# Stationary blocks made contiguous, value products by pairs of heads, and later statistics in a four-block transformer kernel

## The chip, the cores and the metric

The kernel runs on 1 core of a Trainium2 chip. The metric is the device time of one execution in microseconds (us). The kernel before was timed three times: 1725.38, 1725.91 and 1728.11 us, median 1725.91 us.

## The reference, cut to what matters

A sequence of 256 tokens of width 1024, batch 1, in float32, goes through four blocks: a forgetting attention block ("fox"), a block with three sparse attention branches ("nsa"), a block with stick-breaking and dilated attention and a gated feed-forward part ("mixer2", "ffn2"), and a block with pooling, attention and a product-key expert layer ("mixer3", "peer"). Heads have 64 columns; fox and mixer2 have 16 heads. What the change touches:

```python
# fox: every head; c is the running sum of log_sigmoid(f + b_f)
logits = q @ k.T * scale + c[:, None] - c[None, :]        # causal
o = softmax(logits) @ v;   y = (o * silu(z)) @ w_out

# nsa: compress 32 tokens (stride 16) to one key and one value per group
blk = x[16 * i : 16 * i + 32] + pe                        # 32 x 64, flattened to 2048
kc = silu(blk @ w1) @ w2                                  # w1: 2048 x 256

# mixer2, heads 0..7 stick-breaking, 8..15 softmax with a distance bias
log_stay = where(key < query, log_sigmoid(-z), 0)
w = exp(log_sigmoid(z) + sum of log_stay over later keys);  o = w @ v
o = rms_norm_of_each_head(o) * gain
```

All of it starts with a root-mean-square norm of x (in fox: `h = x * rsqrt(mean(x*x)) * g`).

## The kernel before, in words

**Products.** Activations lie transposed in SBUF: 128 rows of a 128-column chunk by 256 tokens (`S`). A float32 product of full accuracy is three float32r products: each operand is split into a high part (rounded to float32r) and a low part (what is left), and hi*hi, hi*lo and lo*hi are summed in PSUM (`mm3`, L448 to L452). Where an operand is handed to TensorE as plain float32, as in `attn_av` (L593 to L596) and in transposes, TensorE makes two passes of it, which are two records in the trace.

**Weights.** `Weights` streams 504 chunks of 128 x 1024 float32 (512 KB): the SP queue loads them into four buffers (`wraw`), ACT makes `whi` (L241), DVE makes `wlo` (L242). There are three pairs of `whi`/`wlo`, and a fourth from another pool for every fourth chunk. `next()` asks for the split of two chunks beyond the one used. In nsa the transfers of `rope` (L632, L633) go through the same SP queue. During mixer2 the queue also brings 48 chunks of `ada`, which DVE reduces (L291), 16 of them among the 16 chunks of the query and key projection.

**Order of the work.** Each stage is a Python generator; `weave` steps the projections ("main") and, at a rate, the attention ("side"), so that TensorE has matmuls of the next weights while a head goes through its softmax. The list so made is then ordered on every engine by the framework's planner, which takes the ready instruction of the earliest place, by its own cost estimates; on the chip each engine runs its list in order. PSUM has four names of two banks each: "pj", "s", "t", "o".

**fox** (0 to 170 us). The projection of the 16 gate columns (`proj(1)`, bank "pj") is evicted by `f_evac` (L666), which first calls `stats()` (L648): ACT squares eight tiles, POOL adds them up (L655), TensorE sums over partitions with a matrix of ones (L657), ACT takes the root, `cols` turns it into a column by two transposes (L444). Then come a few small operations on 16 partitions and, in `c3`, the decay as three bf16 parts. The values follow (`proj_nat(2)`, 8 chunks, banks "s" and then "pj", matmuls of 512 columns, L496 to L498), evicted by ACT (`v_evac`, L696) into `vN` in float32. Then queries and keys are projected in 8 steps of two chunks (`qk_evac`, L701, into one tile for all heads; `stack`, L522, builds float32r operands). For each head `attn_scores` (L548) makes four float32r matmuls and two bf16 ones of 128 and 256 columns that add the decay (L556; the stationary operand is one column of `sel`, repeated 128 times), softmax and norm run on DVE and ACT, three transposes go to PSUM (L584 to L586), DVE copies them out (`ptw`, L588), `attn_av` multiplies by 64 columns of `vN`, and after each odd head `gated` (L605) multiplies by the gate and splits.

**nsa** (170 to 368 us). `blocks()` (L809) adds the position table to `Z`, in which the 8 places of a block lie next to each other, and splits the sum into `zh` and `zl`. `compress` (L824) takes, for each of 16 places j, every eighth column from j on as stationary operand (L830) and multiplies it with 256 columns of `w1` in three products (L832 to L834): 2 x 16 x 3 = 96 matmuls over 8 weight chunks.

**mixer2** (368 to 486 us). Values as in fox (L1070), then the 8 steps of queries and keys woven with 16 heads. A stick-breaking head has two bf16 matmuls of 128 columns for the mask (L1119), a chain of ACT and DVE operations, two float32 matmuls with a triangle (L1136, L1137) and an exponential straight to `ptw` (L1139) without transposes; a dilated head goes as in fox, with its norm on POOL. `finish` (L1083) copies the pair out of PSUM, squares, sums by head on TensorE, and splits. mixer3 has attention too, with `attn_av` as it is.

Of the kernel before, what the change touches and what calls it, by code (L numbers as in the profile page):

```python
# [270 lines left out]
def program(tc, A, out, upto=99):  # L271
    nc = tc.nc
    ctx = ExitStack()
    with ctx:
# [322 lines left out]

        def resid(nxt):
# [42 lines left out]
        def fox(st1):  # L641
            sel = ph.tile([P, NH], BF, name="sel")
# [20 lines left out]
            c3 = ph.tile([P, S], BF, name="c3")  # L663
            nc.vector.memset(c3, 0.0)

            def f_evac(c0, p, m):  # L666
# [16 lines left out]
                for i in range(3):  # L683
                    sl = c3[32 * i:32 * i + NH, :]
                    nc.vector.tensor_copy(sl, r)
                    if i < 2:
                        b = ph.tile([NH, S], F32, name="f6", bufs=2)
                        nc.vector.tensor_copy(b, sl)
# [4 lines left out]
            vN = ph.tile([P, 2, D], F32, name="vN")  # L693
# [4 lines left out]
            qk = ph.tile([P, 8, 2, S], F32, name="qk")  # L698

            def qk_evac(c0, p, m):  # L700
                nc.vector.tensor_tensor(qk[:, c0 // 2], p, rqk, op=OP.mult)  # L701
                stacks[c0 // 2] = stack(qk[:, c0 // 2, 0, :], qk[:, c0 // 2, 1, :])
                cnt["qk"] = c0 // 2 + 1
# [5 lines left out]
            def fox_attn():  # L709
                st = {}  # L710
                po = {}
                for i in range(NH + 3):
# [10 lines left out]
                    if 2 <= i <= NH + 1:  # L723
                        h = i - 2
                        if h % 2 == 0:
                            po[h // 2] = ps.tile([P, S], F32, name="o")
                        attn_av(po[h // 2][(h % 2) * 64:(h % 2) * 64 + 64, :], st[h],
                                lambda kb: vN[:, kb, h * 64:h * 64 + 64])
                        if h % 2 == 1:
                            while cnt["z"] <= h // 2:  # L730
                                yield
                            gated(og, h // 2, po[h // 2], sz)
                        yield

            drain(proj(1, hx, f_evac))
# [14 lines left out]
        def nsa(st1):  # L750
# [58 lines left out]
            def blocks():  # L809
                his = ph.tile([P, 2, 1040], F32R, name="zh", tag="bufA")  # L810
                los = ph.tile([P, 2, 1040], F32R, name="zl", tag="bufB")
                for ab in range(2):
                    t = ph.tile([P, 1040], F32, name="zt", bufs=2)
                    for n, w in ((0, 512), (1, 528)):
                        nc.vector.tensor_tensor(
                            t[:, 512 * n:512 * n + w].rearrange("p (c j) -> p c j", j=8),
                            Z[:, 512 * n:512 * n + w].rearrange("p (c j) -> p c j", j=8),
                            pek[:, n, ab * 8:ab * 8 + 8][:, None, :].to_broadcast([P, w // 8, 8]), op=OP.add)
# [228 lines left out]
        def mixer2(st1):  # L1047
# [19 lines left out]
            vN = ph.tile([P, 2, D], F32, name="vN")  # L1067

            def v_evac(c, tb, p):
                nc.scalar.mul(vN[:, tb, c * 512:c * 512 + 512], p, rc[:, tb:tb + 1])  # L1070

            qk = ph.tile([P, 8, 2, S], F32, name="qk")

            def qk_evac(c0, p, m):
                c = c0 // 2
                nc.vector.tensor_tensor(qk[:, c], p, rqk[:, c // 4], op=OP.mult)
                q, k = qk[:, c, 0, :], qk[:, c, 1, :]
# [5 lines left out]
            def finish(c, po):  # L1083
                o = ph.tile([P, S], F32, name="fo", bufs=2)
                nc.scalar.copy(o, po)
                sq = wk.tile([P, S], F32, name="sq")
                nc.scalar.activation(sq, po, AF.Square)
# [9 lines left out]
            def attn():  # L1097
                st, po = {}, {}

                def av(h):  # L1100
                    if h % 2 == 0:
                        po[h // 2] = ps.tile([P, S], F32, name="o")
                    attn_av(po[h // 2][(h % 2) * 64:(h % 2) * 64 + 64, :], st[h],
                            lambda kb: vN[:, kb, h * 64:h * 64 + 64])
                    if h % 2 == 1:
                        finish(h // 2, po[h // 2])

                for i in range(19):
                    if i < 16:
# [22 lines left out]
                    if 1 <= i <= 16:  # L1132
                        h = i - 1
                        if h < 8:
# [9 lines left out]
                    if 2 <= i <= 17:  # L1144
                        av(i - 2)
# [569 lines left out]
```

## Time and profile before

| | |
|---|---|
| median of 3 runs (lowest, highest) | 1725.91 us (1725.38, 1728.11) |
| the profiled execution's own time | 1728.64 us |
| its span, first to last instruction | 1726.9 us |
| mean granted TensorE clock | 0.993 |
| PE busy | 1680.3 us, 97% |
| weight loads (PEld) busy | 1545.8 us, 90% |
| DVE busy | 1294.4 us, 75% |
| ACT busy | 959.2 us, 56% |
| POOL busy | 185.7 us, 11% |
| read from HBM | 296 MB, 172 GB/s over the span |

Busy time is the time in which an engine had at least one instruction under way. TensorE pipelines matmuls, so the record of one matmul (0.28 us for 256 columns) is longer than the distance to the next; how fast it goes is read from the distance between starts. A bracket behind a row of the timeline tells how long the engine was idle before it and what ended the idle time.

### The profile page before, as it was taken

What the parts mean: (1) busy time and instruction counts of PE and PEld (TensorE: products, weight loads), DVE (VectorE), ACT (ScalarE), POOL (GpSimd) and SP (SyncE); (2) the same over time, 40 slices, a digit from 0 to 9 for tenths busy, and PEclk for the clock granted to TensorE, in tenths of its full rate; (3) what the DMA queues carried; (4) which work ended last, traced back from release to release, by engine and by line L of the source; (5) the groups of instructions that cost most, each with busy time, mean ns of one, the idle gap of its engine ahead of it and who ended that gap; (6) DMA issues with size and microseconds to landing.
All of it is one profiled execution on the core that took longest, in us unless ns stands there. A gap on an engine that the chain in (4) does not pass through costs nothing.

```text
span 1726.9 us, 31770 instructions
## 1 busy us (share of the span) xinstructions
PE 1680.3 (97%) x12108; PEld 1545.8 (90%) x12108; DVE 1294.4 (75%) x2691; ACT 959.2 (56%) x1813; POOL 185.7 (11%) x198
## 2 busy tenths in 40 slices
PE   8999999999999999999999999999999999999997
PEld 6999897788879999889989999999999988888886
DVE  5787767788867766777667987888999666666665
ACT  5666555656855545566644555554444555555554
POOL 2000133531130000111037000000000000000000
PEclk9999999999999999999999999999999999999999
DMA  6434542177527777434544454444444555555553
GB/s 229 144 125 150 170 144 93 63 251 267 190 99 242 258 260 244 138 128 169 186 157 163 163 163 163 158 157 156 161 160 154 173 193 195 195 194 191 193 192 120
DMA packets 84089, 300.08 MB, mean 174 GB/s; under 512 B 10144, under 2 KB 11040, under 8 KB 83680
## 3 DMA queue, kind: packets, MB, share of 16 engines
q1 hardware_dynamic: 83360, 296.39, 51.4%
q8 instruction: 95, 1.56, 0.4%
q10 hardware_dynamic: 576, 1.66, 0.3%
q14 instruction: 58, 0.48, 0.1%
HBM read 296.04 MB, written 1.05 MB: 172 GB/s over the span
## 4 chain that ended last, share of the span: by engine, by line
PE 52%; DVE 3%; ACT 1%; issue 0%; POOLq 0%; POOL 0%; DVEq 0%; ACTq 0%
PE s L1592 10%; PE t L1592 10%; PE pj L450 5%; PE pj L451 5%; PE pj L452 5%; PE o L1552 3%; PE s L450 2%; PE t L450 2%; PE s L452 2%; PE s L451 2%; PE t L451 2%; PE t L452 2%; DVE wlo L242 1%; PE s L1401 0%; PE o L595 0%
## 5 line engine op out<-in xcount | busy, mean ns | idle before, releaser
L242 DVE TENSOR_TENSOR wlo<-wraw,whi 128x1024 fp32r<-128x1024 f32 x486 | 601.9, 1241 | 194.1 <-ACT whi L241 192.3
L241 ACT CAST whi<-wraw 128x1024 fp32r<-128x1024 f32 x504 | 528.6, 1051 | 385.6 <-PE pj L451 124.4
L450 PE MATMUL pj<-hxh,whi 128*128 128x256 f32 x1456 | 422.8, 291 | 5.7 <-ACT vN L1070 1.9
L452 PE MATMUL pj<-hxh,wlo 128*128 128x256 f32 x1456 | 412.3, 284 | 1.9 <-DVE wlo L242 1.4
L451 PE MATMUL pj<-hxl,whi 128*128 128x256 f32 x1456 | 413.1, 284 | 0.6 <-DVE hxl L1161 0.4
L450 PEld LDWEIGHTS pj<-hxh,whi 128*128 128x128 f32 x1456 | 278.2, 191 | 14.0 <-issue 4.8
L452 PEld LDWEIGHTS pj<-hxh,wlo 128*128 128x128 f32 x1456 | 277.5, 191 | 3.8 <-DVE wlo L242 2.2
L451 PEld LDWEIGHTS pj<-hxl,whi 128*128 128x128 f32 x1456 | 277.8, 191 | 2.3 <-DVE hxl L1161 1.1
L1592 PE MATMUL s<-whi,hxl 128*128 128x512 f32 x512 | 157.8, 389 | 0.0
L1592 PE MATMUL t<-whi,hxl 128*128 128x512 f32 x512 | 157.6, 389 | 0.0
L1580 ACT CAST hxl<-a 128x256 fp32r<-128x256 f32 x128 | 52.1, 408 | 152.1 <-PE t L1592 150.3
L450 PE MATMUL s<-hxh,whi 128*128 128x256 f32 x456 | 130.9, 287 | 1.7 <-DVE st L572 1.7
L452 PE MATMUL s<-hxh,wlo 128*128 128x256 f32 x456 | 129.3, 283 | 0.4 <-DVE wlo L242 0.4
L451 PE MATMUL s<-hxl,whi 128*128 128x256 f32 x456 | 128.9, 283 | 0.0
L450 PE MATMUL t<-hxh,whi 128*128 128x256 f32 x424 | 121.4, 286 | 0.0
L452 PE MATMUL t<-hxh,wlo 128*128 128x256 f32 x424 | 119.7, 282 | 0.9 <-DVE wlo L242 0.8
L451 PE MATMUL t<-hxl,whi 128*128 128x256 f32 x424 | 119.5, 282 | 0.0
L1592 PEld LDWEIGHTS t<-whi,hxl 128*128 128x128 f32 x512 | 96.1, 188 | 19.9
L1592 PEld LDWEIGHTS s<-whi,hxl 128*128 128x128 f32 x512 | 95.9, 188 | 20.0 <-ACT hxl L1580 0.2
L1581 DVE TENSOR_TENSOR hxl<-a,hxl 128x256 fp32r<-128x256 f32 x128 | 54.4, 425 | 62.6 <-PE t L1592 60.6
L450 PEld LDWEIGHTS s<-hxh,whi 128*128 128x128 f32 x456 | 87.0, 191 | 2.3 <-issue 2.3
L452 PEld LDWEIGHTS s<-hxh,wlo 128*128 128x128 f32 x456 | 86.9, 191 | 1.1 <-DVE wlo L242 0.8
(396 smaller groups left out, 3373.1 us busy)
## 6 DMA issues: line engine op xcount, KB each, us to landing
wraw<-in_pu SPq DMA_DIRECT2D x128, 512.0 KB
wraw<-in_pv SPq DMA_DIRECT2D x128, 512.0 KB
wraw<-in_b_ffn SPq DMA_DIRECT2D x66, 512.0 KB
wraw<-in_ada SPq DMA_DIRECT2D x48, 512.0 KB
wraw<-in_b_qk SPq DMA_DIRECT2D x24, 512.0 KB
wraw<-in_fox_qk SPq DMA_DIRECT2D x16, 512.0 KB
wraw<-in_b_o SPq DMA_DIRECT2D x16, 512.0 KB
wraw<-in_b_g SPq DMA_DIRECT2D x16, 512.0 KB
```

Of the source, the lines that this page charges most:

```text
L241: nc.scalar.copy(hi, r)
L242: (nc.gpsimd if self.np in self.on_pool else nc.vector).tensor_tensor(lo, r, hi.bitcast(F32), op=OP.subtract)
L450: nc.tensor.matmul(o, wh, xh, start=start, stop=False)
L451: nc.tensor.matmul(o, wh, xl, start=False, stop=False)
L452: nc.tensor.matmul(o, wl, xh, start=False, stop=stop)
L1552: nc.tensor.matmul(p[:, t, :], x[:, w[0], :, w[1]], y[i][:, w[0], :, w[1]], start=i == 0 and t == 0, stop=i == 2, skip_group_check=True)
L1580: nc.scalar.copy(ah, src)
L1581: nc.vector.tensor_tensor(al, src, ah.bitcast(F32), op=OP.subtract)
L1592: nc.tensor.matmul(acc[tb][h], x[:, t], w[:, h * 512:h * 512 + 512], start=n == 0 and i == 0, stop=n == P - 1 and i == 2)
```

## The change

In nsa the 8 places of a block are no longer neighbours: each place's 130 columns lie together. In fox the statistics and the gate columns' eviction run at the first eviction of the values, and the gate projection takes bank "t". In fox and mixer2 values and probabilities are split into float32r high and low parts, and two heads share one product: 128 stationary columns of values, and both heads' probabilities as moving columns; of the result each head's own 64 rows are used. The decay (fox) is float32r and added by one matmul of 512 columns, the mask of the stick-breaking heads by one bf16 matmul of 256 columns. The tile of queries and keys holds one step and has two buffers.

```diff
 # attn_scores
-                n = P + P * qb
-                mm_stack(s[:, qb * S:qb * S + S], st2, e, qb, lambda x: x, True, bias_mm is None)
-                if bias_mm is not None:
-                    nc.tensor.matmul(s[:, qb * S:qb * S + n], bias_mm[0], bias_mm[1][:, 0:n], start=False, stop=True)
+                mm_stack(s[:, qb * S:qb * S + S], st2, e, qb, lambda x: x, bias_mm is None or qb == 0, bias_mm is None, bias_mm is not None)
+            if bias_mm is not None:
+                nc.tensor.matmul(s, bias_mm[0], bias_mm[1][:, None, :].to_broadcast([P, 2, S]), start=False, stop=True,
+                                 skip_group_check=True)
...
+        def values(dst, c, p, r):
+            hi, lo = (t[:, c[0], c[1]] for t in dst)
+            nc.scalar.mul(hi, p, r)
+            nc.vector.scalar_tensor_tensor(lo, p, r, hi.bitcast(F32), op0=OP.mult, op1=OP.subtract)
+        def probs(pt, h, src):
+            if h % 2 == 0:
+                pt[h // 2] = [ph.tile([P, 2, 384], F32R, name=n, bufs=2) for n in ("pth", "ptl")]
+            hi, lo = (t[:, h % 2, :] for t in pt[h // 2])
+            nc.scalar.copy(hi, src)
+            nc.vector.tensor_tensor(lo, src, hi.bitcast(F32), op=OP.subtract)
...
+        def pair_av(pt, v, c):
+            o = ps.tile([P, 2, S], F32, name="o")
+            hi, lo = pt
+            for kb in range(2):
+                q = slice(0, S) if kb == 0 else slice(S, S + P)
+                vh, vl = (t[:, kb, c] for t in v)
+                for i, (w, x) in enumerate(((vh, hi), (vl, hi), (vh, lo))):
+                    nc.tensor.matmul(o[:, :, kb * P:], w, x[:, :, q], start=kb == 0 and i == 0, stop=kb == 1 and i == 2)
+            return o
...
+        def gated_pair(og, c, o, sz):
+            t = wk.tile([P, S], F32, name="sp")
+            for e, a in enumerate(HALF):
+                nc.vector.tensor_tensor(t[a], o[a, e, :], sz[a, c, :], op=OP.mult)
+            split(og, c, t)
...
 # fox
+            vN = [ph.tile([P, 2, D], F32R, name=n) for n in ("vh", "vl")]
             def v_evac(c, tb, p):
-                nc.scalar.mul(vN[:, tb, c * 512:c * 512 + 512], p, rc[:, tb:tb + 1])
+                if held:
+                    f_evac(*held.pop())
+                values(vN, (tb, slice(c * 512, c * 512 + 512)), p, rc[:, tb:tb + 1])
...
-                        st[i - 1] = attn_transpose(st[i - 1])
+                        probs(pt, i - 1, transposed(st[i - 1]))
...
+                    if i >= 3 and i % 2 == 1:
+                        c = (i - 3) // 2
+                        o = pair_av(pt.pop(c), vN, slice(c * P, c * P + P))
...
-            drain(proj(1, hx, f_evac))
+            held = []
+            drain(proj(1, hx, lambda *a: held.append(a), banks=("t",)))
             drain(proj_nat(2, hx, v_evac, ("s", "pj")))
...
 # nsa: blocks, compress
-                            t[:, 512 * n:512 * n + w].rearrange("p (c j) -> p c j", j=8),
+                            t.rearrange("p (j c) -> p j c", j=8)[:, :, 64 * n:64 * n + w // 8],
...
-                        v = [t[:, j:j + 1024].rearrange("p (gc j) -> p gc j", j=8)[:, :, 0] for t in zp[j // 8]]
+                        o = j % 8 * 130 + j // 8
+                        v = [t[:, o:o + P] for t in zp[j // 8]]
...
 # mixer2: finish, stick-breaking heads
-                nc.scalar.copy(o, po)
+                for e, a in enumerate(HALF):
+                    nc.scalar.copy(o[a], po[a, e, :])
...
-                                nc.tensor.matmul(z[:, o:o + P], sbm[:, 0, :], sbm[:, 1, :], start=False, stop=kb == 1,
-                                                 skip_group_check=True)
+                            nc.tensor.matmul(z.rearrange("p (b k) -> p b k", b=2)[:, :, 0:P], sbm[:, 0, :],
+                                             sbm[:, 1, :][:, None, :].to_broadcast([P, 2, P]), start=False, stop=True,
+                                             skip_group_check=True)
...
-                            st[h] = w
+                            probs(pt, h, w)
                         else:
-                            st[h] = attn_transpose(st[h])
+                            probs(pt, h, transposed(st[h]))
```

`transposed` is `attn_transpose` without the copy out of PSUM. The values of nsa and mixer3 stay float32.

## Rows read from the trace of the kernel before

**Rows 1.** Timeline, 10 to 26 us: start, length, engine, line, instruction, tiles, [idle before].

```profile
10.41 7.90 POOL L655 TENSOR_TENSOR acc<-acc,sq 128x256 f32<-128x256 f32 x6 [4.13 <-ACT sq L654]
...
18.37 1.22 PE L657 MATMUL o<-acc,ones 128*128 128x256 f32 x2 [3.87 <-POOL acc L655]
...
20.24 0.63 PE L497 MATMUL s<-wlo,hxh 128*128 128x512 f32 x1
...
20.67 0.63 PE L498 MATMUL s<-whi,hxl 128*128 128x512 f32 x1
...
24.88 0.40 PE L497 MATMUL s<-wlo,hxh 128*128 128x512 f32 x1
...
25.11 0.39 PE L498 MATMUL s<-whi,hxl 128*128 128x512 f32 x1
```

**Rows 2.** Timeline of PE in fox, 97 to 102 us.

```profile
97.32 0.28 PE L452 MATMUL pj<-hxh,wlo 128*128 128x256 f32 x1
97.52 0.65 PE L595 MATMUL o<-ptw,vN 128*64 128x256 f32 x2
98.00 0.38 PE L596 MATMUL o<-ptw,vN 128*64 128x128 f32 x2
...
98.54 0.28 PE L451 MATMUL pj<-hxl,whi 128*128 128x256 f32 x1
98.66 0.28 PE L452 MATMUL pj<-hxh,wlo 128*128 128x256 f32 x1
...
100.54 0.28 PE L545 MATMUL s<-stc,str 128*128 128x256 f32 x1
...
101.39 0.28 PE L451 MATMUL pj<-hxl,whi 128*128 128x256 f32 x1
```

**Rows 3.** Timeline of PE in nsa, at the first products of compress.

```profile
214.05 0.41 PE L832 MATMUL o<-whi,zh 128*128 128x256 f32 x1
214.29 0.40 PE L833 MATMUL o<-wlo,zh 128*128 128x256 f32 x1
```

**Rows 4.** Groups by line, weight loads: count, busy us, mean ns, idle before.

```profile
L450 PEld LDWEIGHTS pj<-hxh,whi 128*128 128x128 f32 x1456 | 278.2, 191 | 14.0 <-issue 4.8 <-ACT vN L1070 2.4 <-ACT hxh L1160 1.6
L832 PEld LDWEIGHTS o<-whi,zh 128*128 128x128 f32 x32 | 10.8, 338 | 0.0
```

**Rows 5.** Windows: stretch, length, busy PE, PEld, DVE, ACT, POOL; clock, DMA, GB/s.

```profile
12.00:34.00 22.00, 17.60 (x66) 13.68 (x65) 14.03 (x24) 10.74 (x17) 6.14 (x6) 0.84 0.59 210
48.00:149.00 101.00, 100.44 (x774) 91.04 (x773) 82.05 (x210) 65.67 (x154) 5.25 (x5) 1.00 0.38 128
214.00:240.00 26.00, 26.00 (x120) 25.80 (x120) 14.98 (x34) 13.65 (x26) 3.82 (x5) 1.00 0.43 142
240.00:349.00 109.00, 101.79 (x766) 87.82 (x765) 84.43 (x302) 66.30 (x192) 51.12 (x72) 1.00 0.27 90
395.00:440.00 45.00, 44.10 (x318) 38.79 (x316) 40.06 (x65) 34.68 (x73) 0.00 (x0) 0.99 0.78 262
440.00:486.00 46.00, 45.58 (x315) 38.32 (x315) 35.29 (x92) 34.20 (x95) 9.31 (x16) 1.00 0.39 134
```

**Rows 6.** Groups by line on DVE and ACT.

```profile
L242 DVE TENSOR_TENSOR wlo<-wraw,whi 128x1024 fp32r<-128x1024 f32 x486 | 601.9, 1241 | 194.1 <-ACT whi L241 192.3
L241 ACT CAST whi<-wraw 128x1024 fp32r<-128x1024 f32 x504 | 528.6, 1051 | 385.6 <-PE pj L451 124.4 <-issue 97.7 <-PE t L451 30.5
L588 DVE COPY ptw<-t 128x384 f32<-128x384 f32 x48 | 26.4, 550 | 5.7 <-PE t L586 5.4
L588 ACT COPY ptw<-t 128x384 f32<-128x384 f32 x16 | 7.6, 474 | 9.1 <-PE o L596 8.0 <-PE t L586 0.9
L607 DVE TENSOR_TENSOR sp<-o,sz 128x256 f32<-128x256 f32 x16 | 6.8, 424 | 16.0 <-PE o L596 12.1 <-POOL sz L616 3.8
L701 DVE TENSOR_TENSOR qk<-pj,rqk 128x512 f32<-128x512 f32 x8 | 5.5, 690 | 3.6 <-PE pj L452 3.6
```

**Rows 7.** Timeline of PE in mixer2, after the values.

```profile
392.01 0.39 PE L450 MATMUL pj<-hxh,whi 128*128 128x256 f32 x1 [1.93 <-ACT vN L1070]
```

More of the change, by code (lines that the diff above doesn't have):

```diff
@@ L596, in attn_av, with transposed @@
             nc.tensor.matmul(o[:, 128:256], v(1), pt[:, 256:384], start=False, stop=stop)
+        def values(dst, c, p, r):
[8 more added lines that the diff above has]
+            nc.vector.tensor_tensor(lo, src, hi.bitcast(F32), op=OP.subtract)
+        def transposed(pn):
+            p = ps.tile([P, 384], F32, name="t")
+            for i in range(3):
+                nc.tensor.transpose(p[:, i * P:i * P + P], pn[:, i * P:i * P + P], ident)
+            return p
+        def pair_av(pt, v, c):
[7 more added lines that the diff above has]
+            return o
         def resid(nxt):
@@ L641, in fox @@
         def fox(st1):
-            sel = ph.tile([P, NH], BF, name="sel")
+            sel = ph.tile([P, NH], F32R, name="sel")
             nc.gpsimd.tensor_copy(sel, C["sel"])
@@ L661, in stats @@
                 rc = cols(rstd)
-            c3 = ph.tile([P, S], BF, name="c3")
-            nc.vector.memset(c3, 0.0)
+            c3 = ph.tile([P, S], F32R, name="c3")
+            nc.vector.memset(c3.bitcast(F32), 0.0)
             def f_evac(c0, p, m):
@@ L709, in fox_attn @@
             def fox_attn():
-                st = {}
-                po = {}
+                st, pt = {}, {}
                 for i in range(NH + 3):
@@ L720, in fox_attn @@
                     if 1 <= i <= NH:
-                        st[i - 1] = attn_transpose(st[i - 1])
+                        probs(pt, i - 1, transposed(st[i - 1]))
                         yield
[L723 to L732, printed above, removed]
+                    if i >= 3 and i % 2 == 1:
+                        c = (i - 3) // 2
+                        o = pair_av(pt.pop(c), vN, slice(c * P, c * P + P))
+                        while cnt["z"] <= c:
+                            yield
+                        gated_pair(og, c, o, sz)
                         yield
-            drain(proj(1, hx, f_evac))
+            held = []
+            drain(proj(1, hx, lambda *a: held.append(a), banks=("t",)))
             drain(proj_nat(2, hx, v_evac, ("s", "pj")))
@@ L815, in blocks @@
                         nc.vector.tensor_tensor(
-                            t[:, 512 * n:512 * n + w].rearrange("p (c j) -> p c j", j=8),
-                            Z[:, 512 * n:512 * n + w].rearrange("p (c j) -> p c j", j=8),
-                            pek[:, n, ab * 8:ab * 8 + 8][:, None, :].to_broadcast([P, w // 8, 8]), op=OP.add)
+                            t.rearrange("p (j c) -> p j c", j=8)[:, :, 64 * n:64 * n + w // 8],
+                            Z[:, 512 * n:512 * n + w].rearrange("p (c j) -> p j c", j=8),
+                            pek[:, n, ab * 8:ab * 8 + 8][:, :, None].to_broadcast([P, 8, w // 8]), op=OP.add)
                     hi, lo = his[:, ab, :], los[:, ab, :]
@@ L1065, in mixer2 @@
                 nc.gpsimd.tensor_scalar(xT[:, kt, :], xT[:, kt, :], V["gf"][:, kt:kt + 1], ALPHA, op0=OP.mult, op1=OP.mult)
-            vN = ph.tile([P, 2, D], F32, name="vN")
+            vN = [ph.tile([P, 2, D], F32R, name=n) for n in ("vh", "vl")]
             def v_evac(c, tb, p):
-                nc.scalar.mul(vN[:, tb, c * 512:c * 512 + 512], p, rc[:, tb:tb + 1])
-            qk = ph.tile([P, 8, 2, S], F32, name="qk")
+                values(vN, (tb, slice(c * 512, c * 512 + 512)), p, rc[:, tb:tb + 1])
             def qk_evac(c0, p, m):
                 c = c0 // 2
-                nc.vector.tensor_tensor(qk[:, c], p, rqk[:, c // 4], op=OP.mult)
-                q, k = qk[:, c, 0, :], qk[:, c, 1, :]
+                qk = ph.tile([P, 2, S], F32, name="qk", bufs=2)
+                nc.vector.tensor_tensor(qk, p, rqk[:, c // 4], op=OP.mult)
+                q, k = qk[:, 0, :], qk[:, 1, :]
                 stacks[c] = stack(k, q) if c < 4 else stack(q, k)
@@ L1097, in attn @@
             def attn():
[L1098 to L1106, printed above, removed]
+                st, pt = {}, {}
                 for i in range(19):
@@ L1139, in attn @@
                             nc.scalar.activation(w, z[:, 0:384], AF.Exp)
-                            st[h] = w
+                            probs(pt, h, w)
                         else:
-                            st[h] = attn_transpose(st[h])
+                            probs(pt, h, transposed(st[h]))
                         yield
-                    if 2 <= i <= 17:
-                        av(i - 2)
+                    if i >= 3 and i % 2 == 1 and i <= 17:
+                        c = (i - 3) // 2
+                        finish(c, pair_av(pt.pop(c), vN, slice(c * P, c * P + P)))
                         yield
```

11 lines of the change are left out of this document (5 added, 6 removed).

## The prediction

> **What bounds the kernel now.** I read the shares of busy time first: TensorE has something under way in 97% of the span, so only time taken off TensorE's list, or a stall of it, can move the end. Busy is not fast, so the timeline of PE came next, read by distances between starts. At full clock a float32r matmul of 512 columns takes 0.23 us (24.88 to 25.11 [rows 1]), one of 256 columns 0.12 us (98.54 to 98.66 [rows 2]). Anything slower than that per column is a target, and three of the four edits sit on such places. The windows by stage came last [rows 5]: they say how much room DVE and ACT have in the stages where PE would get shorter. In fox DVE is busy 82.05 of 101 us, in the two halves of mixer2 it is 40.06 of 45 and 35.29 of 46 us, and ACT 34.68 and 34.20. Mixer2 is the stage with little room.
>
> **Compress (nsa).** 96 matmuls of 256 columns stand 0.24 us apart (214.05 to 214.29 [rows 3]) where other matmuls of this size stand 0.12 apart. The cause is in the weight loads: 338 ns for the stationary operand with a step of 8 elements, 191 ns for a contiguous one [rows 4]. With contiguous blocks I take the ordinary distance: 96 x (0.2425 - 0.1185) = 11.9 us. Can the weights follow? A chunk is then used up in 12 x 0.1185 = 1.42 us, against 1.05 us of ACT and 1.24 us of DVE to split it [rows 6]; three split chunks and up to four loaded ones are in hand when compress begins, and DVE is busy 14.98 of 26 us there [rows 5], 8 x 1.24 = 9.9 of it with these splits. So five splits must follow in about 11 us, which fits; I take off 1 us for waits: 10.9. Bounds: 11.9, and 4 if what follows cannot start earlier (a rival below). The additions of the table now read with a step of 8 and may take longer on DVE; doubling all four (about 0.7 us each by a 512-column addition [rows 6]) costs 2.8 us of DVE. A projection stands between them and compress, so I count 0; without that cover it is the 2.8.
>
> **Statistics later (fox).** [...] The splits of the third and later chunks no longer stand behind the statistics on ACT. Gain 3.87 + 2.0 = 5.9 us. [...] The gate columns' small DVE operations go with the statistics; the first head needs them only after the first step of queries and keys. SP's queue gets earlier loads, nothing else.
>
> **Values in two parts.** Each eviction of the values gets a DVE operation from PSUM of 512 columns, 0.69 us by the nearest row (L701 [rows 6]), four a stage. Only the last ones show, because the next projection needs bank "pj": in mixer2 PE already waits 1.93 us for ACT there [rows 7]. One operation more makes 0.7 if DVE is free, and 0.7 + 1.24 if a `wlo` stands before it. I take 0.7 in fox and 1.0 in mixer2, where DVE is fuller: -1.7 us. Bounds -1.4 and -3.9.
>
> **Products by pairs (fox and mixer2).** One head's `attn_av` shifts the stream from 97.32 + 0.12 to 98.54 - 0.12: 0.98 us [rows 2], 1.96 for a pair. A pair then has three matmuls of 512 and three of 256 columns: 3 x 0.23 + 3 x 0.12 = 1.05 us. Saved 0.91 to 0.93 a pair, 7.4 us for the 8 pairs of each stage. The second key block writes 128-column runs into both halves of the bank, and no row shows such a product; from both sides it is 0.12 (a contiguous one) and 0.24 us (the slowest of this size [rows 3]), over 24 matmuls a stage 0 to 2.9 us; I take 0, as runs of 128 are nearer to the contiguous row.
> [...]
>
> **Decay and mask.** In fox six matmuls of a head, four of them float32r of 256 columns, take 100.54 to 101.39 - 0.12 = 0.73 us [rows 2], so the two bf16 ones take 0.73 - 0.47 = 0.26. One float32r matmul of 512 columns takes 0.23: 16 x 0.03 = 0.4 us (between 0 and 1). For the mask I take the same 0.26 now, and 0.13 with one matmul: 8 x 0.13 = 1.0 us.
>
> **What the pairs cost elsewhere.** Fox: DVE's copy of the transposed probabilities (0.55 us) becomes a subtraction, about as long; new are ACT copies of 384 columns, 16 x 0.47 = 7.6 us [rows 6], on an ACT busy 65.67 of 101 us, and a second `gated` half, 8 x 0.42 = 3.4 us of DVE. DVE then has 85.4 us; at the highest share it reaches with PE near full (40.06/45 = 89% [rows 5]) that takes 96.0 us, where PE alone would take 101 - 7.8 = 93.2. So between 5.0 and 7.8 us stay; I take 6.3.
> Mixer2: DVE gets 8 subtractions for heads that had none (8 x 0.55 = 4.4), in all 75.35 + 4.4 = 79.75 of 91 us; ACT gets 16 copies and 8 halves in `finish`, 16 x 0.47 + 3 = 10.5, in all 79.4. PE alone would take 91 - 8.4 = 82.6 us, which asks 97% of DVE and 96% of ACT. At 89% DVE needs 89.6. So of 8.4 us I keep 1.0; bounds 8.4, and -4 if the half with the stick-breaking heads, where DVE is at 89% already, stretches by the 4.4 us without anything given back.
>
> **Sum.** 10.9 + 5.9 - 1.7 + 6.3 + 1.0 = 22.4 us. The profiled execution took 1728.64 us in all (span 1726.9 and 1.7 around it): 1706.2. It lies 2.7 us above the median of the runs, 1725.91, so I forecast 1703.5 us for the median. The likeliest case's own range is 1698 to 1709.
>
> **Rivals.** (1) All of TensorE's saving stays, because engines run closer than 89% with the planner's new order: 11.9 + 5.9 + 7.8 + 8.4 - 1.4 = 32.6, 1693 us. For it: PE waits for almost nothing in fox and mixer2 now. Against it: the 97% above.
> (2) Compress is faster, but the heads of nsa start no earlier, as their chain goes through SP's transfers for the rotation and POOL's norms: from 240 to 349 us PE has 7 us without work [rows 5], so the stage is partly bound by that chain. 4 of 10.9 us stay: 1710.5 us. Against it: 101.8 us of PE work stand in that window, which do start earlier.
> (3) The later statistics don't happen on the chip: the planner places the sum before the values, and the stall stays: 5.9 less, 1709.5 us.
> (4) Products whose result lies in two runs go at the distance of 0.24: 48 products and 8 masks, 56 x 0.12 = 6.9 us: 1710.5 us. [...]
> (5) Slower than before: in mixer2 the DVE subtraction of each pair stands behind two `wlo` and two `ada` operations, and `pair_av` is at the head of PE's list and waits. [...] For it: DVE at 89%. Against it: heads run two steps ahead, and PE is without work for only 0.9 and 0.4 us in the two windows now [rows 5].
>
> **Chances.** Forecast 0.46; rivals (1) 0.18, (2) 0.15, (3) 0.08, (4) 0.05, (5) 0.08. A difference under 0.2% (3.5 us) can't be told from no change. Cases one to four and the forecast are faster: 0.92; of (5) I give 0.05 to slower and 0.03 to within 0.2%. The range of 1692 to 1713 us holds all cases but (5) and the mishaps that add up.
>
> **What would show it.** Right: L832 to L834's successors 0.12 us apart and done about 12 us after they begin; no wait of the ones matmul, clock 1.00 from 12 to 34 us; a pair's products within 1.05 us; DVE over 89% in mixer2 with PE waits for `ptl` or `wlo`. Wrong: the distance in compress still 0.24; the window of 109 us after compress growing by what compress gave; mixer2 shorter by 8 us, or longer than before.

## The result, and the profile after

The changed kernel takes 1714.88 us (median of 5 runs, 1713.54 to 1719.51) against 1726.43 us (5 runs, 1725.38 to 1730.87): ratio 0.9938, 95% interval 0.9925 to 0.9952, or 10.7 us less (8.3 to 12.9). The forecast was 1703.5 us, and 1714.88 us lies above its range of 1692 to 1713 us. The sign is right; half of the 22.4 us did not come. Two more sets of runs of the same kernel gave 0.9937 (0.9918 to 0.9956) and 0.9929 (0.9913 to 0.9945).

The profiled execution has a span of 1713.1 us, 13.8 less than before, and TensorE's busy time falls by 22.2 us (1680.3 to 1658.1): it has 8.4 us more without work. Busy times of the page, engine by engine:

```profile
span 1713.1 us, 31723 instructions
PE 1658.1 (97%) x12052; PEld 1532.3 (89%) x12052; DVE 1304.1 (76%) x2715; ACT 976.3 (57%) x1853; POOL 189.4 (11%) x198
```

The windows of after that answer to [rows 5], in its columns:

```profile
12.00:34.00 22.00, 22.00 (x99) 18.08 (x98) 17.37 (x24) 13.70 (x20) 8.00 (x6) 0.97 0.78 268
37.30:140.00 102.70, 100.06 (x789) 96.60 (x790) 88.78 (x223) 73.07 (x172) 6.14 (x6) 1.00 0.43 135
208.00:222.00 14.00, 14.00 (x118) 13.72 (x116) 13.35 (x26) 11.92 (x23) 2.21 (x2) 1.00 0.74 263
222.00:335.00 113.00, 104.69 (x763) 89.77 (x762) 85.11 (x310) 67.38 (x194) 52.06 (x74) 0.97 0.27 87
380.00:427.00 47.00, 44.77 (x324) 40.42 (x325) 43.77 (x74) 38.99 (x84) 0.43 (x1) 1.00 0.74 245
427.00:475.00 48.00, 43.47 (x307) 38.45 (x306) 36.92 (x95) 40.50 (x107) 8.27 (x16) 1.00 0.42 140
```

The first row is the start: TensorE now has work in all of the 22 us, where it had 17.60. The third is compress: 14 us instead of 26, with DVE at 95%. The fourth, the heads of nsa, has grown from 109 to 113 us, at a granted clock of 0.97 where it was 1.00. The last two are mixer 2: TensorE is without work for 2.2 and 4.5 us, where it was 0.9 and 0.4.

The single steps, in the timeline of PE of after: two products of compress, the products of a pair in fox, the matmul over the squares, and the first product after mixer 2's values.

```profile
208.03 0.28 PE L870 MATMUL o<-whi,zh 128*128 128x256 f32 x1
208.15 0.28 PE L871 MATMUL o<-wlo,zh 128*128 128x256 f32 x1
...
86.48 0.39 PE L628 MATMUL o<-pth,vh 128*128 128x512 f32 x1
86.72 0.40 PE L628 MATMUL o<-pth,vl 128*128 128x512 f32 x1
86.95 0.39 PE L628 MATMUL o<-ptl,vh 128*128 128x512 f32 x1
87.18 0.28 PE L628 MATMUL o<-pth,vh 128*128 128x256 f32 x1
87.30 0.28 PE L628 MATMUL o<-pth,vl 128*128 128x256 f32 x1
87.41 0.28 PE L628 MATMUL o<-ptl,vh 128*128 128x256 f32 x1
87.53 0.28 PE L450 MATMUL pj<-hxh,whi 128*128 128x256 f32 x1
...
24.32 0.59 PE L696 MATMUL o<-acc,ones 128*128 128x256 f32 x2
...
380.35 0.39 PE L450 MATMUL pj<-hxh,whi 128*128 128x256 f32 x1 [3.42 <-DVE vl L602]
```

Compress goes at 0.12 instead of 0.24 [rows 3]. A pair takes 87.53 - 86.48 = 1.05 us, as worked out from [rows 1, 2]. The matmul over the squares waits for nothing. The last row is a new cost: 3.42 us of waiting for the low part of the values, where it was 1.93 [rows 7].

How far after is ahead of before at the same instruction of both traces (differences of start times):

| place | ahead by, us |
|---|---|
| last product of fox's values | 5.8 |
| first product of fox's queries and keys | 4.8 |
| last gating of fox | 9.4 |
| first addition of a block in nsa | 8.7 |
| first split of a block in nsa | 8.3 |
| first, last product of compress | 6.0, 17.8 |
| last gating of nsa | 13.5 |
| first product of mixer 2's queries and keys | 11.7 |
| finish of mixer 2's 5th pair | 18.5 |
| finish of mixer 2's 8th pair | 10.8 |
| end | 13.8 |

Every edit takes time off where it stands, and some of it is given back ahead of compress, in nsa, and in mixer 2, at the values and again from the fifth pair on.

### The profile page after: what moved, and what is told of

The parts are those of the page before. It is cut to its first block, busy times and chain, and to the rows that moved or that the text cites. A ratio compares the mean times of both kernels' runs of the same rounds, so it can differ in the third digit from the quotient of the medians.

```text
span 1713.1 us, 31723 instructions
## 1 busy us (share of the span) xinstructions
PE 1658.1 (97%) x12052; PEld 1532.3 (89%) x12052; DVE 1304.1 (76%) x2715; ACT 976.3 (57%) x1853; POOL 189.4 (11%) x198
## 3 DMA queue, kind: packets, MB, share of 16 engines
HBM read 296.04 MB, written 1.05 MB: 173 GB/s over the span
## 4 chain that ended last, share of the span: by engine, by line
PE 52%; DVE 3%; ACT 0%; issue 0%; POOLq 0%; POOL 0%; DVEq 0%; ACTq 0%
PE s L1624 10%; PE t L1624 10%; PE pj L450 5%; PE pj L451 5%; PE pj L452 5%; PE o L1584 3%; PE s L450 2%; PE t L450 2%; PE s L452 2%; PE s L451 2%; PE t L451 2%; PE t L452 2%; DVE wlo L242 1%; PE s L1433 0%; PE o L595 0%
## 5 line engine op out<-in xcount | busy, mean ns | idle before, releaser
L242 DVE TENSOR_TENSOR wlo<-wraw,whi 128x1024 fp32r<-128x1024 f32 x486 | 601.1, 1241 | 168.2 <-ACT whi L241 165.7
L450 PE MATMUL pj<-hxh,whi 128*128 128x256 f32 x1448 | 417.0, 288 | 7.0 <-DVE vl L602 4.5
L450 PEld LDWEIGHTS pj<-hxh,whi 128*128 128x128 f32 x1448 | 276.4, 191 | 11.6 <-DVE vl L602 5.4
L291 DVE SCALAR_TENSOR_TENSOR wraw<-wraw,cb 128x1024 f32<-128x1024 f32 x48 | 59.6, 1241 | 44.5 <-DMA wraw<-in_ada 44.2
```

The costliest lines, as they stand in the source:

```text
L242: (nc.gpsimd if self.np in self.on_pool else nc.vector).tensor_tensor(lo, r, hi.bitcast(F32), op=OP.subtract)
L291: nc.vector.scalar_tensor_tensor(t, t, 1.0, cb, op0=OP.mult, op1=OP.mult, accum_out=modT[:, i:i + 1])
L450: nc.tensor.matmul(o, wh, xh, start=start, stop=False)
```

## The experiments

### One part at a time

Four kernels start from the one before and take one part each: the contiguous blocks; the later statistics; the pairs with the two-part values in fox, then in mixer 2 (both without the edits of decay and mask).

```
e1:  o = j % 8 * 130 + j // 8;  v = [t[:, o:o + P] for t in zp[j // 8]]   # and the additions that write so
e2:  drain(proj(1, hx, lambda *a: held.append(a), banks=("t",)))          # f_evac from the first v_evac
e3:  values, probs, pair_av, gated_pair in fox
e4:  values, probs, pair_av, two halves in finish in mixer2
```

> Only the contiguous key blocks of nsa, everything else as before. Theory A (nsa gives back most of what compress saves: the slower strided additions on DVE hold up the gates' transposes, about 2.7 us, and the heads after compress start no earlier, about 4.2 us): compress 11.8 us shorter, the whole 4 to 6 us faster. Rival B (these losses were the low clock of one execution, in three stretches of nsa, and not a rule): 9 to 11 us faster in the median of the runs.

> Only the later statistics of fox, with the gate projection in bank t. Theory A (each edit acts for itself): the wait for POOL's sums goes and the low clock shortens, 5 to 6 us faster, and all of it stays to the end. Rival (what is won at the start is waited for later, as the splits on DVE and ACT set the pace of fox): less than 3 us faster.

> Only fox's values and probabilities in two parts with products by pairs; decay in bf16, statistics, compress and mixer2 as before. Theory A (TensorE saves 7.4 us, about 2 go to the eviction of the values and 2 to waits for DVE and ACT): 3 to 5 us faster. Rival (in the full change fox lost to the other edits, as the earlier start): 6 to 7 us faster.

> Only mixer2's values and probabilities in two parts with products by pairs, and the smaller tile of queries and keys; mask as before. Theory A (ACT and DVE are full there, so TensorE's 7.4 us come back as waits, most of them in the half with the dilated heads): within 2 us of the kernel before, with ACT over 80% and PE waits ahead of the transposes. Rival (mixer2 gains by itself and lost only beside the other edits): 5 to 7 us faster.

| part | forecast gain, us | measured ratio (interval) | gain, us |
|---|---|---|---|
| blocks | 10.9 | 0.9955 (0.9936 to 0.9973) | 7.8 (4.7 to 11.0) |
| statistics | 5.9 | 0.9971 (0.996 to 0.9983) | 5.0 (2.9 to 6.9) |
| pairs in fox | 6.3 - 0.4 (decay) - 0.7 = 5.2 | 0.9967 (0.9956 to 0.9979) | 5.7 (3.6 to 7.6) |
| pairs in mixer 2 | 1.0 - 1.0 = 0.0 | 1.0012 (1.0001 to 1.0023) | -2.1 (-4.0 to -0.2) |

Gains are one minus the ratio, by the 1725.4 us of before in these runs. Three parts hold their forecasts within their intervals, the blocks only near the upper end. The statistics came as theory A has it; the intervals of the blocks and of fox's pairs reach into both of their theories. Mixer 2's pairs alone make the kernel slower, close to what theory A has, with 4.1 us of waits ahead of the transposes.

### The change without mixer 2's pairs

All else stays as changed; mixer 2 goes back to float32 products head by head and one-part values.

```
-  vN = [ph.tile([P, 2, D], F32R, name=n) for n in ("vh", "vl")]
+  vN = ph.tile([P, 2, D], F32, name="vN")
-  finish(c, pair_av(pt.pop(c), vN, slice(c * P, c * P + P)))
+  av(i - 2)                       # attn_av of one head, as before
```

> The changed kernel with mixer2's values, probabilities and products in float32 by single heads as before; the mask in one matmul and the small tile of queries and keys stay. Theory A (pairs in mixer2 cost 2.1 us, alone as well as here): 2 to 4 us faster than the changed kernel. Rival (beside the other edits they are worth their 7.4 us of TensorE, or nothing): 0 to 7 us slower than the changed kernel.

> The change with mixer 2's products as before, once more, on the chip of the two runs before it. If the 0.9904 of the earlier run was this version's own time: 0.989 to 0.992. If it was a lucky set of executions: 0.9925 or above, and then mixer 2's pairs cost no more than the 2 us that they cost alone.

> The changed kernel as it is, once more, beside the kernel before on one chip. The parts alone gave 7.8, 5.0 and 5.7 us less and 2.1 us more, in all 16.4 us less by the ratios. Theory A (the parts add up, and the first measurement of 10.7 us was on its low side): 13 to 16 us faster. Rival (parts of the change get in each other's way, as at the gates of nsa and at the values of mixer2): 9 to 12 us faster.

Measured: 1708.32 us, 0.9904 (0.9885 to 0.9922), and again 1708.85 us, 0.9898 (0.9881 to 0.9914). The change beside them: 0.9937 (0.9918 to 0.9956). So mixer 2's pairs cost some 0.0034 in the change, 5.9 us, more than the 2 to 4 us of theory A, and this version beats both kernels: 16.6 and 17.6 us below before. The second set shows that the first was no lucky one. The change beside it gained 10.9 us where its parts alone add up to 16.4: the rival, that parts get in each other's way, and not theory A.

### Which heads, and what of them

```
e11:  if c == 0: values(vN, ...)   else: nc.scalar.mul(v1[:, tb, :], p, ...)   # pairs for heads 0 to 7, the stick-breaking ones
e12:  if c == 1: ...                                                          # pairs for heads 8 to 15, the dilated ones
```

> The change with pairs in mixer 2 for the eight stick-breaking heads only; the dilated heads' products in float32, head by head, as before. Without any pairs in mixer 2: 0.9904; with all: 0.9938. Theory A (the dilated half is where the pairs lose, as the finishes of the profile say: 7 us given back after the fifth): the ratio is near that without pairs, or below it by what the stick-breaking half gains, 0.988 to 0.991. Theory B (the loss is that of the values and splits common to both halves): half way, 0.9915 to 0.9925. Theory C (the stick-breaking half is what loses, since its gain is given back anyway): 0.993 to 0.994.

> The mirror of the run before it: pairs in mixer 2 for the eight dilated heads only, the stick-breaking heads in float32, head by head. Theory A: the dilated pairs carry the loss, 0.993 to 0.996. Theory B: half way, 0.9915 to 0.9925. Theory C: near that without pairs, 0.990 to 0.991.

Measured: stick-breaking heads only 0.9926 (0.9911 to 0.9942), dilated heads only 0.9913 (0.9893 to 0.9933). Theory A, that the dilated pairs carry the loss, doesn't fit the first of these; between halves (B) and stick-breaking pairs (C) the times alone don't decide. The stage decides. The finishes of the table above lose in the dilated half, but what makes them lose is the pairs of the other half. These are windows from the first product of mixer 2's values to the last of its output projection (columns as in [rows 5]), one fence for each of before, after, without pairs, stick-breaking only and dilated only:

```profile
365.50:504.20 138.70, 134.41 (x897) 116.41 (x896) 115.19 (x208) 89.81 (x196) 37.20 (x39) 0.99 0.62 208
```

```profile
352.00:493.00 141.00, 129.44 (x872) 114.05 (x870) 119.33 (x220) 100.59 (x220) 35.46 (x39) 1.00 0.62 203
```

```profile
349.20:487.60 138.40, 132.44 (x889) 114.38 (x889) 113.46 (x209) 90.65 (x196) 36.78 (x39) 1.00 0.63 206
```

```profile
352.60:494.10 141.50, 133.29 (x881) 116.65 (x880) 117.62 (x218) 95.39 (x207) 35.76 (x39) 0.98 0.63 203
```

```profile
352.20:490.20 138.00, 131.91 (x880) 116.46 (x878) 113.45 (x210) 95.21 (x207) 34.84 (x39) 0.98 0.62 207
```

With all pairs TensorE has 3.0 us less under way than without (132.44 to 129.44, both at clock 1.00) and 11.6 us without work instead of 6.0: the stage is longer, not shorter. One profile each could mislead, since the stage varies by some 2 us between executions, so here is its length in more profiles:

| pairs in mixer 2 | rest of the kernel | length of the stage, us |
|---|---|---|
| none | as before, then with one of the other three parts each | 138.7, 139.0, 139.2, 136.8 |
| none | as changed, twice, then with the blocks added on GpSimd (below) | 138.4, 138.0, 136.7 |
| dilated heads | as changed | 138.0 |
| stick-breaking heads | as changed | 141.5 |
| all | as before | 142.8 |
| all | as changed, three times, then with the blocks added on GpSimd | 141.0, 142.9, 142.1, 141.5 |

With pairs for the dilated heads the stage is as long as without any; with pairs for the stick-breaking heads it is some 4 us longer, as it is with all pairs (and 140.0 to 143.1 in the kernels below that have them). It is so beside the old rest (142.8 against 138.4 on average) and beside the new one (141.9 against 137.7). The granted clock is 0.96 to 1.00 in these windows, and does not sort them: at 1.00 there are 141.0 with all pairs and 136.7 to 139.2 without.

The next kernels try the suspects one by one. A first wait, that for the low values at 380.35, is removed by giving the values another bank:

```
-  drain(proj_nat(2, hx, v_evac, ("s", "pj")))
+  drain(proj_nat(2, hx, v_evac, ("s", "t")))
```

> The changed kernel with the second half of mixer2's values in bank t in place of pj, so that the first projection of queries need not wait for the eviction in two parts. Theory A (this wait, 3.4 us of PE, costs what it lasts): the wait goes, 2 to 4 us faster than the changed kernel. Rival (the weights' splits or the loads are late there anyway): the wait moves to another releaser, under 1 us.

Measured: 0.9938 (0.9921 to 0.9956), no change. The wait is gone (the first query product starts 18.6 us ahead of before instead of 11.7), but until the last chunk's eviction 9.4 us of this lead are given back, where after gives back 4.6. Removing this wait was worth nothing, as the rival has it.

Then ScalarE: the dilated heads' high parts go to DVE.

```
+  probs(pt, h, transposed(st[h]), nc.vector.tensor_copy)
```

> The changed kernel with the high part of the dilated heads' probabilities copied by DVE in place of ACT, 8 copies of 0.47 us off ACT and 8 of 0.55 us onto DVE. Theory A (the half with the dilated heads is slower because ACT is the engine that is full there, with 40 of 48 us, and its queue delays the exponentials): 1 to 4 us faster than the changed kernel. Rival (the chain from scores to transposes is delayed by DVE and POOL as much, or the chain itself is too long for two heads ahead): no change or slower.

Measured: 0.9937 (0.9921 to 0.9953), no change, as the rival has it. Then DVE's subtraction for the stick-breaking heads, and their copy too, go to GpSimd:

```
e13:  probs(pt, h, w, nc.gpsimd.tensor_tensor)
e14:  probs(pt, h, w, nc.gpsimd.tensor_tensor, nc.gpsimd.tensor_copy)
```

> The whole change, with the subtraction for the stick-breaking heads' low parts (8 of 384 columns) on GpSimd in place of VectorE. Theory A (VectorE's added work is the cost): the 3.8 us of the stick-breaking pairs go, and the ratio falls from 0.9938 to 0.991 to 0.992. Theory B (the pair's later order, or ScalarE): 0.993 to 0.9945. Theory C (GpSimd is too slow, or it slows VectorE): above 0.9945.

> As the run before, and the copy for the high parts of these heads on GpSimd too, so that the pairs add nothing to VectorE or ScalarE in the stick-breaking half but the halves of finish. Theory A: as the run before, 0.991 to 0.992. Theory A2 (ScalarE's copies cost as well): below it, 0.989 to 0.9905. Theory B (the order): 0.993 to 0.9945. Theory C (GpSimd's two steps of a head come late): above 0.9945, with waits of TensorE for the pairs' parts.

Measured: 0.9949 (0.9933 to 0.9964) and 0.9942 (0.9925 to 0.9958). No gain in either. That looks like a verdict against DVE as the cause, and is none. Groups of DVE and POOL from 387 to 460 us, of after and then of the first of the two:

```profile
L242 DVE TENSOR_TENSOR wlo<-wraw,whi 128x1024 fp32r<-128x1024 f32 x15 | 18.3, 1218 | 2.1 <-ACT whi L241 2.0
L291 DVE SCALAR_TENSOR_TENSOR wraw<-wraw,cb 128x1024 f32<-128x1024 f32 x12 | 14.6, 1218 | 0.1
...
L611 DVE TENSOR_TENSOR ptl<-ptw,pth 128x384 fp32r<-128x384 f32 x8 | 4.4, 553 | 0.1
```

```profile
L242 DVE TENSOR_TENSOR wlo<-wraw,whi 128x1024 fp32r<-128x1024 f32 x15 | 19.0, 1274 | 1.2 <-ACT whi L241 1.1
L291 DVE SCALAR_TENSOR_TENSOR wraw<-wraw,cb 128x1024 f32<-128x1024 f32 x13 | 18.0, 1388 | 0.4 <-DMA wraw<-in_ada 0.3
...
L611 POOL TENSOR_TENSOR ptl<-ptw,pth 128x384 fp32r<-128x384 f32 x8 | 11.1, 1383 | 48.4 <-ACT pth L610 43.5 <-issue 4.9
```

DVE lost 4.4 us of subtractions and got 15 x 0.056 + 13 x 0.170 = 3.1 us back in these two groups, and 1.5 us more in the two splits of `stack` (420 to 469 and 418 to 478 ns on average, 14 of each), since some of its operations grew longer beside GpSimd's. So the last two kernels leave the work out instead of moving it. The first computes no low parts for the stick-breaking heads (the third product repeats the second); in the other the exponential also writes the high part itself, so that ScalarE's copy is gone too. Their outputs lack that small term, and in the second the probabilities of these heads are rounded.

```
e16:  (vh, lo) if low else (vl, hi)            # no subtraction for heads 0 to 7
e17:  nc.scalar.activation(pt[h // 2][0][:, h % 2, :], z[:, 0:384], AF.Exp)
```

> The change without the low parts of the probabilities of the eight stick-breaking heads: the subtraction is left out, and the third product of a pair repeats the second, so that TensorE's list is as long as before; the output lacks that small term. VectorE has 4.4 us less in that half, GpSimd nothing more. Theory A (VectorE's added work is the cost): ratio 0.991 to 0.992, 3 us or more below the change. Theory B (ScalarE's copies or the later order of the pairs): 0.993 to 0.9945, as the change.

> As the run before, and the exponential of these heads writes the float32r part itself, so that ScalarE's copy of 384 columns is left out too (rounded probabilities, no low parts). The pairs then add nothing in this half but the vl of the values and the second half of each finish. Theory A: as the run before, 0.991 to 0.992. Theory A2 (ScalarE's copies count as well): 0.9885 to 0.9905, at or below the version without pairs. Theory B2 (the order, products later than head by head): 0.993 to 0.9945.

> The change as it is, for comparison on the same chip: 0.993 to 0.9945.

Measured: 0.9941 (0.9926 to 0.9956), 0.993 (0.9913 to 0.9947), and the change beside them 0.9929 (0.9913 to 0.9945). So DVE's subtraction is not what theory A takes it for: its 0.991 to 0.992 lies outside the first interval. With ScalarE's copy gone too, theory A2 is out (0.9885 to 0.9905), but the second interval still reaches into theory A's 0.991 to 0.992, and the stage takes 140.0 us (140.9 in the first) against 141.0 to 142.9 in the change: a microsecond or two of the 4 may lie in these two operations, the rest does not. What remains of the list is the order of the work, the low parts of the values, and the longer `finish` (two copies, and a square that waits for them); the kernel with dilated pairs only has the last two for its own heads, at 138.0 us. Waits of PE from 350 to 492 us, of after and of the version without pairs (columns: engine, bank, line, releaser: us in total, times, longest):

```profile
PE pj L450 <- DVE vl L602: 3.4, 1, 3.4
PE t L616 <- POOL pn L578: 3.2, 3, 1.4
```

```profile
PE s L545 <- ACT str L534: 2.2, 1, 2.2
PE pj L450 <- ACT vN L1108: 1.7, 1, 1.7
```

The new wait is that of the dilated heads' first transposes for their norms (L578). It is there in the other kernels with stick-breaking pairs too (1.6 us with these pairs only, 1.6 and 1.7 us in the two that leave work out, 4.1 us with mixer 2's pairs alone). With dilated pairs alone it is 0.2 us. In the kernels with stick-breaking pairs the last chunk of queries and keys is evicted 78 to 83 us after the first product of these projections (85 in the one with the other bank), against 73 to 76 in those without and in before, and less is left to do behind it. My reading is that the stick-breaking heads run ahead, the projections fall back, and when the dilated heads begin TensorE has to wait for their chain. It is read from the traces and not shown: no run set the order by hand.

### The additions of the blocks

```
-  nc.vector.tensor_tensor(t.rearrange("p (j c) -> p j c", j=8)[...
+  nc.gpsimd.tensor_tensor(t.rearrange("p (j c) -> p j c", j=8)[...
```

> The whole change, with the four strided additions of the key blocks on GpSimd in place of VectorE. Theory A (my 'I count 0' for these additions failed): VectorE is what the gates' transposes wait for, 2.85 us with the change against 1.76 before; with the additions gone from it that wait falls to 1.8 us or less, the low clock that follows at 191 us goes with it, and the time is 2 to 4 us below the change's: ratio to before 0.9915 to 0.9925. Theory B: GpSimd is slower at them, the blocks come later than the compress products want them, and the wait moves there: ratio 0.994 or above, with a wait of over 1 us ahead of the first compress product. Theory C: the additions were never on the path: 0.9938 within 0.001 and the wait at the gates as it was.

> Mixer 2's products as in the kernel before (float32, head by head), everything else as changed, and the blocks' additions on GpSimd. The change without mixer 2's pairs stood at 0.9904. Theory A: the gates' wait goes, 2 to 4 us less: 0.988 to 0.9893. Theory B or C (wait moved, or never on the path): 0.9895 to 0.9915.

Measured: 0.9957 (0.9942 to 0.9972) and, without mixer 2's pairs, 0.9917 (0.9901 to 0.9932): theory A is wrong, GpSimd makes it worse or no better. The additions and the wait of PE for the gates behind them, first before, then after, then the first of these two kernels:

```profile
L815 DVE TENSOR_TENSOR zt<-Z,pek 128x528 f32<-128x528 f32 x2 | 1.3, 702 | 0.0
L815 DVE TENSOR_TENSOR zt<-Z,pek 128x512 f32<-128x512 f32 x2 | 1.3, 686 | 0.0
...
198.60 0.44 PE L797 MATMUL t<-ident,g 128*128 128x128 f32 x2 [1.76 <-ACT g L508]
```

```profile
L852 DVE TENSOR_TENSOR zt<-Z,pek 128x528 f32<-128x528 f32 x2 | 2.4, 1233 | 0.5 <-DMA Z<-xd 0.5
L852 DVE TENSOR_TENSOR zt<-Z,pek 128x512 f32<-128x512 f32 x2 | 2.2, 1140 | 0.0
...
191.01 0.69 PE L833 MATMUL t<-ident,g 128*128 128x128 f32 x2 [2.85 <-ACT g L508]
```

```profile
L852 POOL TENSOR_TENSOR zt<-Z,pek 128x512 f32<-128x512 f32 x2 | 3.2, 1643 | 28.6 <-DMA Z<-xd 28.6
L852 POOL TENSOR_TENSOR zt<-Z,pek 128x528 f32<-128x528 f32 x2 | 2.8, 1434 | 4.6 <-DMA Z<-xd 4.6
...
192.21 0.69 PE L833 MATMUL t<-ident,g 128*128 128x128 f32 x2 [4.46 <-ACT g L508]
```

The additions stand on DVE's list ahead of what makes the gates, but they are not all of the longer wait. It is 2.2 us with the blocks alone, and 2.5 us with fox's pairs alone, whose additions are those of before. There the second pair of additions starts late, as it does in after (0.5 us) and in the change's third profile (1.3 us, with a wait of 4.1 us for the gates); in before and with the blocks alone it doesn't wait. The late start and the wait for the gates, with fox's pairs alone:

```profile
182.83 1.33 DVE L846 TENSOR_TENSOR zt<-Z,pek 128x528 f32<-128x528 f32 x2 [0.61 <-DMA Z<-xd]
...
196.24 0.44 PE L828 MATMUL t<-ident,g 128*128 128x128 f32 x2 [2.48 <-ACT g L508]
```

What it waits for is a transfer into `Z`; why that lands later beside fox's pairs is not shown. Behind the longer wait TensorE's clock is lower too: the windows there, of before and of after. That the wait brings the low clock is not shown: behind the 3.42 us at 380.35 the clock is 1.00 (380.3 to 390 us).

```profile
198.00:203.00 5.00, 4.39 (x20) 3.66 (x21) 3.14 (x6) 2.28 (x4) 0.00 (x0) 1.00 0.50 169
```

```profile
191.00:196.00 5.00, 4.99 (x16) 4.11 (x17) 2.90 (x5) 1.05 (x1) 0.00 (x0) 0.67 0.48 140
```

From the gates to the first product of compress it is 15.4 us in before and 15.5 with the blocks alone or fox's pairs alone, but 17.0 us in after.

## Why the prediction was right or wrong, point by point

- **Compress: right where it stands, too large in the sum.** The step from the first to the last product fell by 11.8 us (alone 11.1), and the weight loads from 338 to 189 ns [rows 4]. The bound was 11.9; the 1 us for late splits was not needed in after, with DVE at 95% in that window.
- **"A projection stands between them and compress, so I count 0": failed.** The strided additions take 1.14 and 1.23 us instead of 0.69 and 0.70, and between the first of them and the first product of compress the change loses 8.7 - 6.0 = 2.7 us (3.0 and 3.9 in its other two profiles). But the blocks alone lose 0.4 there and fox's pairs alone 0.8: the loss is that of both together. In after 1.1 us of it are the longer wait for the gates and 1.6 TensorE's lower clock behind it (0.67 from 191 to 196 us), a term that the text did not have. The 2.8 us that it named as the price without cover is of this size by luck, since it was worked out from DVE's time.
- **Rival (2), the heads of nsa start no earlier: mostly wrong.** Behind compress 4.2 us were given back in after's profile, most of it to the clock. From the last product of compress to the last value product of nsa's heads after takes 112.8 us at 0.97; the version without mixer 2's pairs has the same instructions at 1.00 (a window around them):

```profile
222.00:332.00 110.00, 101.69 (x763) 87.50 (x763) 85.19 (x310) 68.16 (x196) 52.19 (x73) 1.00 0.28 89
```

  There the way takes 109.7 us. Before has 108.5 at 1.00, and the kernels with only the statistics or only fox's pairs, whose nsa is that of before, 111.4 and 111.5 at 0.97. So at either clock 1.2 to 1.4 us of the 11.8 are given back; the heads do start earlier.
- **Statistics: right.** 5.0 us alone, 5.9 forecast; the stall is gone, and rival (3) with it. Of the 5.9, no run shows the 2.0 us: what the trace of before shows behind the wait of 3.87 us [rows 1] is a granted clock of 0.50 from 18 to 22 us and seven distances of 0.42 to 0.43 us between 19.81 and 23.65, which is 7 x 0.20 = 1.4 us. In after the clock of the start is 0.97, in the kernel with the statistics alone 1.00.
- **Fox: right in the times, a little high in the step.** Alone, the pairs gave 5.7 us (3.6 to 7.6) against 5.2. Between the first query product and the last gating 4.5 us came off in after, under the 5.0 that I gave as the lower bound; the evictions of the values cost 1.0 instead of 0.7. DVE is at 86% (88.78 of 102.7 us), under the 89% that I took for its ceiling; what PE waits for instead, 2.6 us there, are the heads' stacks and norms.
- **Products in two runs, rival (4): wrong here.** The second key block's products, in two runs of 128 columns, start 0.12 us apart (87.18, 87.30, 87.41, 87.53), like contiguous ones of this size (0.12 in [rows 2]).
- **Mixer 2, "of 8.4 us I keep 1.0": the main step that failed.** With 1.0 taken off for the values the term was 0; it measures -2.1 us alone and about -5.9 in the change, and in the stage about -4 both times. The lower bounds, -4 and the 1.0, make -5. The size of the saving on TensorE's list was right pair by pair (1.04 to 1.06 us for the pairs that nothing interrupts), but it never became time. The reason given was wrong too: I divided DVE's work by a share of 89% (91 - 89.6 leaves 1.4, not 1.0). DVE reached 93% (43.77 of 47 us), and taking its 4.4 us of subtractions out gave nothing clear of noise. What the sum had no term for is TensorE's time without work, 11.6 us of the stage instead of 6.0, which comes with the pairs of the stick-breaking heads and not with those of the dilated ones. The bound of -4 had the right heads and the size, but its reason, DVE's 4.4 us, is at most a part. Rival (5), PE waiting for the subtraction at each head, is not what happened: no wait of that kind is among PE's waits in after; the waits are for the values' low part (3.4 us) and the norms (3.2). The sign of being right that named waits for `ptl` or `wlo` did not come either (0.4 us for `wlo`).

The accounts: 22.4 us were forecast, 10.7 came. Of the shortfall some 6 us are mixer 2's pairs, as the version without them shows (16.6 and 17.6 us gained). The blocks' measured 7.8 (4.7 to 11.0) for 10.9 is about 3 of the rest, with an interval that leaves from nothing to 6; the traces account for half of it, 0.4 us ahead of compress and some 1.2 us behind it.

Open: what paces mixer 2 at some 138 us without pairs, and by what the pairs of the stick-breaking heads add 4 us to it. The order of heads and projections is the candidate; it was not tried by itself. That the pairs cost 2.1 us alone and 5.9 in the change need not be a difference: in the stage they cost 4.4 and 4.2 us, and both fit the intervals of the times.

## What to carry to other kernels

A matmul stream is shortened where its distance is wide for a cause in its own row (a weight load of 338 ns, a float32 product); that part of the forecast held here (11.8 us for 11.9 in compress, 1.03 to 1.06 for 1.05 a pair). Whether the stage gets shorter is another question: in a stage where the others are near 90%, first ask whether it shortens at all when TensorE's list does, and leave a pairing out of any place where it only adds work and delays a product. Before a stage's length is explained from one profile each, look at how much it varies between profiles of the same work: here by some 2 us, half of the effect. To learn whether an engine's added work costs something, leave the work out rather than move it: the engine that it is moved to can slow the one it came from (here DVE's L291 from 1218 to 1388 ns on average).

## What the runs showed of the hardware

- GpSimd at work makes some of DVE's operations longer: with the stick-breaking heads' subtractions on GpSimd the reduction of `ada` (L291) went from 1218 to 1388 ns on average, the splits (L242) from 1218 to 1274, while the 8 subtractions of 384 columns took 1383 ns each on GpSimd (553 on DVE). It is not spread evenly: in the trace of after the 442 splits with no GpSimd operation beside them take 1223 ns on average and at most 1246, the 44 with one 1418 and up to 2339. DVE's subtractions of 384 columns that read PSUM (`ptl<-t`) kept their time there: 551 ns on average for the 7 with a GpSimd operation beside them, 554 for the other 17.
- A DVE addition whose operand is read with a step of 8 elements, and whose result goes to runs of 64, takes 1140 ns for 512 columns in after, against 686 for the same sum in order in before.
- The same instructions of nsa's heads take 112.8 us at a granted clock of 0.97 in after and 109.7 at 1.00 in the version without mixer 2's pairs. A difference of 3 us between two profiles in such a stage needs the clock column beside it before it is put down to an edit.
